# Two-layer recurrent trunk in fp32: half chunks split ahead of the three passages, and a fixed order of the opening

## The chip, the cores and the metric

The kernel runs on one core of one Trainium2 chip. The metric is the device time of one execution in microseconds (us); lower is better. The time before is the median of three runs.

The engines are named as the profile names them: PE (TensorE, matmul) with its weight load PEld, DVE (VectorE), ACT (ScalarE), POOL (GpSimd) and SP (SyncE, which here only issues transfers).

## The reference, cut to what matters

256 tokens of width 2048 pass through two layers. Each layer has a mixer (HGRN2 in the first, gated linear attention in the second) and a squared-ReLU MLP with an inner width of 8192. Each of these four sub-layers is wrapped in the same way: an RMS norm before, an RMS norm with a weight behind, and a residual addition.

```python
def rmsnorm(x, w):
    xf = x.astype(jnp.float32)
    y = xf * lax.rsqrt(jnp.mean(xf * xf, axis=-1, keepdims=True) + NORM_EPS)
    return (y * w.astype(jnp.float32)).astype(x.dtype)

def reference(x, ...):
    ...
    h = x
    for i in range(DEPTH):
        hn = rmsnorm(h, norm_mix_pre[i])
        j = i // N_MIXERS
        if i % N_MIXERS == 0:
            m = hgrn2_mixer(hn, hgrn_w_in[j], lower_bounds[i], hgrn_norm[j], hgrn_w_out[j])
        else:
            m = gla_mixer(hn, gla_w_in[j], gla_w_gk[j], gla_b_gk[j], gla_norm[j], gla_w_out[j])
        h = h + rmsnorm(m, norm_mix_post[i])
        f = sqrelu_mlp(rmsnorm(h, norm_mlp_pre[i]), mlp_w_up[i], mlp_w_down[i])
        h = h + rmsnorm(f, norm_mlp_post[i])
    return h
```

The time goes into the products with the weights, 430 MB of them read once, all in fp32 accuracy.

## The kernel before

**Products.** Activations and weights are split into a high part that the matmul reads exactly (fp32r) and a low remainder. A weight chunk of 1 MB (tile `raw`, three buffers, `load_chunk`, L98) holds two half chunks of 128 x 1024. ACT copies each half into `hi` (L105) and DVE subtracts it from `raw` to give `lo` (L106); the helper is `split`, and the pool `wsp` has five buffers for `hi` and five for `lo`. `mm_half` then does three matmuls of 128x512 for each of the two 128-row slices `k` of a half chunk: high times high (L120), low weight times high activation (L121), high weight times low activation (L122). `gemmT` (L140, L141) does the same with the weights held still, for results that are wanted transposed. The activations of a stage lie in `Xhl` tiles (`xhl`), a high and a low part for each of 16 slices `k` and two token blocks `t` of 128.

**Passages.** `transition` joins the end of one sub-layer to the start of the next; there are three: from the HGRN mixer to its MLP (about 492 us), from the MLP to the attention mixer (about 1212 us), and from that mixer to the last MLP (about 1615 us). A passage has the last of four output quarters (512 columns each) left to multiply. `last(t, j)` is that product for token block `t` and one of the last four half chunks. Then come the post-norm: `first_use` squares the quarter with a running sum (ACT, L278), `rstd` reduces the sums, takes root and reciprocal (DVE L299, ACT L194, DVE L196), `weigh` multiplies a quarter by the norm weight (DVE, L283), and `residual(n, t)` adds the normed quarter `n` to the running tile `h` (DVE, L304). From `h` follow the next activations: `T(t, q)` transposes four 128x128 blocks on PE (L175), ACT writes the high part (L186) and DVE the low part (L188) of four slices `k`. Meanwhile `split_next` splits the first half chunks of the next weights, named N0 to N7 here, and `nxt(t, j)` multiplies them with the new activations. In a passage six of these eight low parts are made on POOL:

```python
        def split_next(eng=G):
```

The second passage has one step more, since the MLP's output is a running sum over groups: `first_use` adds the product to it first (DVE, L343).

**What sets the order.** The code is written for a tile framework whose scheduler orders the instructions of each engine by priority. Inside a `manual_schedule` block the written order holds for the engines named, and only work from outside the block is put between it. Each engine executes its own list strictly in order, and waits there for the tiles it needs. All transfers are issued on SP's queue, in order; an issue waits until the tile's buffer is free. So the transfer for N4 and N5, which takes the raw buffer of the last own half chunk, can be issued once that half is split.

**Opening.** `start` (the first sub-layer) loads the transposed input `xs` and the first weight half chunks in alternation on SP, the very first in two parts of 512 columns, with the input quarters (tile `h`) between the later half chunks; the scheduler orders the computation. `prew` holds the pre-norm weights. `rrow` brings the reciprocal roots of the input's mean squares into a row by two matmuls (tile `psr`); they stand between the second and the third transposed product there.

Of the kernel before, what the change touches and what calls it, by code (L numbers as in the profile page):

```python
# [18 lines left out]
P = 128  # L19
T = 256  # L20
# [10 lines left out]
def trunk(  # L31
# [24 lines left out]
    nc.sync.dma_start(prew, npre)  # L56
# [13 lines left out]
    A.activation(warm, epsb, AF.Sqrt)  # L70
# [30 lines left out]
    def split(raw, eng=None):  # L101

        hi = wsp.tile([P, 1024], F32R, tag="hi", name=nm("hi"))
        lo = wsp.tile([P, 1024], F32R, tag="lo", name=nm("lo"))
        A.activation(hi, raw, AF.Copy)  # L105
        (eng or V).tensor_tensor(lo, raw, hi.bitcast(F32), ALU.subtract)  # L106
        return hi, lo
# [6 lines left out]
    def mm_half(ps, half, hf, xs, t, nk):  # L114

        hi, lo = (w.rearrange("p (k n) -> p k n", k=2) for w in half)
        for kk in range(2):
            k = 2 * hf + kk
            xh, xl = xs(k, t)
            PE.matmul(ps, xh, hi[:, kk, :], start=(k == 0), stop=False)  # L120
            PE.matmul(ps, xh, lo[:, kk, :], start=False, stop=False)  # L121
            PE.matmul(ps, xl, hi[:, kk, :], start=False, stop=(k == nk - 1))  # L122
# [10 lines left out]
    def gemmT(wap, idx, X):  # L133


        ps = psmm.tile([P, 2, T], F32, tag="mm", name=nm("mmT"))
# [62 lines left out]

    def start(which, w, base):  # L200
# [5 lines left out]
        ps = [psmm.tile([P, NB], F32, tag="mm", name=nm("mm")) for _ in range(NT)]  # L206

        def load_h(t, q):
            c = slice(q * NB, (q + 1) * NB)
            nc.sync.dma_start(h[:, t, c], x[t * P:(t + 1) * P, c])  # L210

        def load_half(c, j):
            nc.sync.dma_start(ahead[c][1][:, j, :], w[c].rearrange("p (k n) -> p k n", k=2)[:, j, :])

        with tc.manual_schedule(engines={mybir.EngineType.SP}):
            for hf in range(KT // 2):
# [3 lines left out]
                if hf >= 4:  # L220
                    load_h(0, hf - 4)
                for n in range(2 if hf == 0 else 1):
# [3 lines left out]
                    cs = slice(n * NB, (n + m) * NB)  # L226
                    nc.sync.dma_start(xs[:, ks, :], xT[:, ks, :])
                    nc.sync.dma_start(raw[:, hf % 2, cs], src[:, hf % 2, cs])
# [12 lines left out]
                for t in range(NT):  # L241
                    mm_half(ps[t], half, hf, X, t, KT)
            for q in range(4):
                load_h(1, q)
            nc.sync.dma_start(ident, ident_in)
            for c in range(2):
                ahead[c] = w, wraw.tile([P, 2, 1024], F32, tag="raw", name=nm("raw"))
                for j in range(2):
                    load_half(c, j)
        return X, token_rstd(), ps  # L250

    def token_rstd():
        part = small.tile([P, NT, 4], F32, tag="tp", name=nm("tp"))
        for t in range(NT):
            for q in range(4):
                A.activation(tok(), h[:, t, q * NB:(q + 1) * NB], AF.Square,
                             accum_out=part[:, t, q:q + 1])
# [5 lines left out]
    def rrow(rs):  # L263
        ps = pssc.tile([P, NT, P], F32, tag="sc", name=nm("psr"))
# [6 lines left out]
    class Post:  # L271
# [8 lines left out]
        def weigh(self, ps, n, t):  # L280

            self.mw[n, t] = tok() if ps.space == PSUM else ps
# [6 lines left out]
        def wp(self, n):  # L289
            if ("w", n) not in self.mw:  # L290
                w = tokp.tile([P, NB], F32, tag="wp", bufs=1, name=nm("wp"))
# [10 lines left out]
        def residual(self, n, t):  # L302
            hs = h[:, t, n * NB:(n + 1) * NB]
            V.scalar_tensor_tensor(hs, self.mw[n, t], self.r[t], hs, ALU.mult, ALU.add)  # L304

    ALL = {mybir.EngineType.PE, mybir.EngineType.Activation, mybir.EngineType.DVE,
           mybir.EngineType.Pool}

    def transition(w, base, nk, xs, post, add, which, wn, nbase):
# [15 lines left out]
        raws, N = [], []  # L325
        psn = [psmm.tile([P, NB], F32, tag="mm", name=nm("mm")) for _ in range(NT)]

        def last(t, j):
            mm_half(ps[t], halves[nh - 4 + j], nh - 4 + j, xs, t, nk)

        def split_next(eng=G):
# [3 lines left out]
            N.append(split(raws[-1][:, j % 2, :], eng))  # L335
# [4 lines left out]
        def first_use(t):  # L340
# [5 lines left out]
            return src  # L346

        def T(t, q):
            pt = transpose4(lambda j: h[:, t, q * NB + j * P:q * NB + (j + 1) * P])
            put_split(pt, X, 4 * q, t, lambda j: prew[:, which, 4 * q + j:4 * q + j + 1])  # L350

        post.wp(n)
        with tc.manual_schedule(engines=ALL):
            for j in range(4):
                last(0, j)
            split_next()
            m0 = first_use(0)
            last(1, 0)
            post.rstd(0)
            split_next()  # L360
            post.residual(0, 0)
            post.residual(1, 0)
            last(1, 1)
            split_next()
            post.weigh(m0, n, 0)
            post.residual(2, 0)
            post.residual(3, 0)
            last(1, 2)
            T(0, 0)
            last(1, 3)  # L370
            m1 = first_use(1)
            ss = col()
            V.tensor_reduce(ss, post.part[1], mybir.AxisListType.X, ALU.add)
            T(0, 1)
            post.r[1] = rstd_of(ss, D, 1)
            split_next()
            post.residual(0, 1)
            post.residual(1, 1)
            nxt(0, 0)
            T(0, 2)  # L380
            nxt(0, 1)
            if add is None:
                T(1, 0)
            nxt(0, 2)
            if add is not None:
                T(1, 0)
            T(1, 1)
            nxt(0, 3)
            split_next()
            post.weigh(m1, n, 1)  # L390
# [473 lines left out]
```

## Time and profile before

| quantity | value |
|---|---|
| median of three runs | 2350.85 us (2349.45 to 2351.37) |
| profiled execution, its own time | 2349.59 us |
| its span, first to last instruction | 2347.4 us |
| mean granted clock of PE | 0.996 |
| PE busy | 2320.2 us, 99% of the span |
| PEld, DVE, ACT, POOL busy | 84%, 65%, 51%, 2% |
| read from memory | 429.59 MB, 184 GB/s over the span |
| POOL's half splits | 18, mean 2591 ns |

The profiled execution stands 1.26 us below the median. Its page lists, for each engine, the busy time and its share of the span; groups of instructions give a line of the kernel, the engine, the operation, output and input tiles, the count, and behind the bar the busy time with the mean duration, and the idle time of that engine just before them with what ended it. A timeline row is start and duration in us, the engine, the line, and in brackets the idle time before it and what ended that. The list of waits gives total, number of times and the longest. Window rows give the stretch, its length, and for each engine the busy time with the number of instructions, then PE's granted clock, the busy share of the transfer engines and GB/s.

### The profile page before, as it was taken

To read this page: it belongs to the slowest core of one execution; us is meant where nothing else is said; L and a number is where in the kernel's file an instruction comes from. 1 tells how busy PE (TensorE), PEld (TensorE's weight loads), DVE (VectorE), ACT (ScalarE), POOL (GpSimd) and SP (SyncE) were. 2 spreads that over 40 slices of the span, in tenths; PEclk is the share of its full clock that TensorE was granted. 3 is DMA by queue.
4 is the path that set the end of the run, shared out by engine and by line. 5 is a ranking of instruction groups with operands and counts; after the bars stand their busy time and mean duration, and the time that the engine had idled before them with its cause. 6 is when DMAs were issued, how large, how long until landed. Compare 5 with 4: busy or idle time off the path is not lost.

```text
span 2347.4 us, 29579 instructions
## 1 busy us (share of the span) xinstructions
PE 2320.2 (99%) x11688; PEld 1960.6 (84%) x11688; DVE 1517.2 (65%) x2091; ACT 1197.6 (51%) x1750; POOL 46.7 (2%) x22
## 2 busy tenths in 40 slices
PE   8999999999999999999999999999999999999998
PEld 7888888878888888888878888887888888888887
DVE  6787777566565565565576767656656556556556
ACT  7454554456454454454447456554645445445443
POOL 0000000020000000000010000002000000000000
PEclk9999999999999999999999999999999999999999
DMA  9544545545555555555554544454555555555553
GB/s 320 180 161 163 178 162 178 173 153 203 192 191 186 197 182 195 190 187 194 184 174 156 207 161 163 162 192 167 198 194 183 198 183 194 188 189 189 190 195 139
DMA packets 65867, 433.61 MB, mean 185 GB/s; under 512 B 7968, under 2 KB 8352, under 8 KB 15168
## 3 DMA queue, kind: packets, MB, share of 16 engines
q1 hardware_dynamic: 65728, 431.71, 53.5%
q8 instruction: 92, 1.51, 0.3%
q14 instruction: 47, 0.39, 0.0%
HBM read 429.59 MB, written 2.10 MB: 184 GB/s over the span
## 4 chain that ended last, share of the span: by engine, by line
PE 96%; DVE 3%; ACT 0%; DMA 0%; SPq 0%; issue 0%; DVEq 0%; ACTq 0%
PE mmT L140 27%; PE mm L121 17%; PE mm L122 17%; PE mm L120 17%; PE mmT L141 14%; PE sc L506 2%; DVE h L304 2%; PE tr L175 1%; DVE xhl L188 1%; PE sd L541 0%; PE po L590 0%; PE po L593 0%; PE po L592 0%; DVE tok L283 0%; DMA raw<-w_hin 0%; ACT xhl L186 0%
## 5 line engine op out<-in xcount | busy, mean ns | idle before, releaser
L106 DVE TENSOR_TENSOR lo<-raw,hi 128x1024 fp32r<-128x1024 f32 x776 | 948.7, 1225 | 711.7 <-ACT hi L105 710.4
L105 ACT ACTIVATE hi<-raw 128x1024 fp32r<-128x1024 f32 x794 | 839.5, 1060 | 986.2 <-PE mm L122 577.5
L140 PE MATMUL mmT<-xhl,hi 128*128 128x512 f32 x2704 | 952.8, 397 | 0.1
L141 PE MATMUL mmT<-xhl,lo 128*128 128x256 f32 x2704 | 761.5, 282 | 0.8 <-DVE lo L106 0.8
L122 PE MATMUL mm<-hi,xhl 128*128 128x512 f32 x1856 | 726.3, 392 | 7.4 <-DVE xhl L188 7.4
L120 PE MATMUL mm<-hi,xhl 128*128 128x512 f32 x1856 | 727.7, 394 | 5.6 <-ACT hi L238 5.6
L121 PE MATMUL mm<-lo,xhl 128*128 128x512 f32 x1856 | 726.8, 392 | 0.4 <-DVE lo L239 0.4
L140 PEld LDWEIGHTS mmT<-xhl,hi 128*128 128x128 f32 x2704 | 507.3, 188 | 121.7 <-issue 1.3
L141 PEld LDWEIGHTS mmT<-xhl,lo 128*128 128x128 f32 x2704 | 510.8, 189 | 3.1 <-DVE lo L106 1.1
L122 PEld LDWEIGHTS mm<-hi,xhl 128*128 128x128 f32 x1856 | 350.0, 189 | 81.8 <-DVE xhl L188 8.7
L120 PEld LDWEIGHTS mm<-hi,xhl 128*128 128x128 f32 x1856 | 350.1, 189 | 77.8 <-ACT hi L238 6.3
L121 PEld LDWEIGHTS mm<-lo,xhl 128*128 128x128 f32 x1856 | 350.3, 189 | 73.0 <-issue 1.0
L106 POOL TENSOR_TENSOR lo<-raw,hi 128x1024 fp32r<-128x1024 f32 x18 | 46.5, 2591 | 1592.3 <-ACT hi L105 1581.5
L149 DVE TENSOR_TENSOR half<-mmT,half 128x256 f32<-128x256 f32 x169 | 70.6, 418 | 0.0
L447 DVE TENSOR_TENSOR tok<-tok,mm 128x512 f32<-128x512 f32 x108 | 69.0, 680 | 0.0
L148 ACT COPY half<-mmT 128x256 f32<-128x256 f32 x169 | 59.7, 354 | 0.0
L433 DVE SCALAR_TENSOR_TENSOR half<-half,rr 128x256 f32<-128x256 f32 x120 | 51.0, 425 | 4.2
L436 ACT ACTIVATE half<-half 128x256 f32<-128x256 f32 x120 | 50.3, 419 | 3.7
L437 DVE TENSOR_TENSOR xhl<-half,xhl 128x256 fp32r<-128x256 f32 x120 | 50.2, 419 | 0.0
L435 ACT ACTIVATE xhl<-half 128x256 fp32r<-128x256 f32 x120 | 48.0, 400 | 0.0
L304 DVE SCALAR_TENSOR_TENSOR h<-tok,col,h 128x512 f32<-128x512 f32 x32 | 47.8, 1531 | 0.3
L570 DVE TENSOR_TENSOR qk<-qk,tt 128x256 f32<-128x256 f32 (+1 forms) x96 | 46.6, 517 | 1.7 <-ACT kc L524 1.7
(132 smaller groups left out, 777.6 us busy)
## 6 DMA issues: line engine op xcount, KB each, us to landing
raw<-w_up SPq DMA_DIRECT2D x128, 1024.0 KB, 4.8
raw<-w_dn SPq DMA_DIRECT2D x128, 1024.0 KB, 4.8
raw<-w_hin SPq DMA_DIRECT2D x58, 1024.0 KB, 4.8
raw<-w_gin SPq DMA_DIRECT2D x48, 1024.0 KB, 4.8
raw<-w_hout SPq DMA_DIRECT2D x16, 1024.0 KB, 4.8
raw<-w_gout SPq DMA_DIRECT2D x16, 1024.0 KB, 5.0
raw<-w_hin SPq DMA_DIRECT2D x11, 512.0 KB, 7.1
wp<-npost SPq DMA_DIRECT2D x16, 256.0 KB, 3.4
```

Of the source, the lines that this page charges most:

```text
L105: A.activation(hi, raw, AF.Copy)
L106: (eng or V).tensor_tensor(lo, raw, hi.bitcast(F32), ALU.subtract)
L120: PE.matmul(ps, xh, hi[:, kk, :], start=(k == 0), stop=False)
L121: PE.matmul(ps, xh, lo[:, kk, :], start=False, stop=False)
L122: PE.matmul(ps, xl, hi[:, kk, :], start=False, stop=(k == nk - 1))
L140: PE.matmul(ps, hi[:, kk * P:(kk + 1) * P], X.both(k), start=(k == 0), stop=False)
L141: PE.matmul(ps[:, 0, :], lo[:, kk * P:(kk + 1) * P], X.both(k)[:, 0, :], start=False, stop=(k == KT - 1))
L148: A.copy(u, ps[:, 1, :])
L149: V.tensor_tensor(u, ps[:, 0, :], u, ALU.add)
L304: V.scalar_tensor_tensor(hs, self.mw[n, t], self.r[t], hs, ALU.mult, ALU.add)
L433: V.scalar_tensor_tensor(u, u, 0.0, rr[0], ALU.max, ALU.mult)
L447: V.tensor_tensor(m[n, t], m[n, t], ps[t], ALU.add)
```

## The change

**Passages.** POOL is no longer used. `split` is cut into `split_hi` (ACT) and `split_lo` (DVE), and six of the next stage's half chunks (N0 to N5) are split ahead of the passage's block. Their parts lie in spare tiles, which the generator `spares` hands out: the feature tiles `qk`, `f` and `tt` (N0, N1), the accumulators (N2), the ordinary pool (N3) and one buffer of `big` (N4, N5). `first_use` now also weighs the quarter. The transposes (`T_in`) and their copies (`T_out`) are separate steps, and PE's order is written anew: all of `nxt(0, j)` stands inside the block, and `nxt(1, j)` follows it.

**Opening.** The order in `start` is written out for all engines. The first `xs` goes first on SP, the first weight part goes on ACT's queue, `prew` comes second; four matmuls on a constant run first on PE; the first half chunk is multiplied slice by slice; the first four transposed products are issued there (`next_chunk`), and the input quarters are loaded among their chunks. `rrow` comes behind the four.

**Weight quarter.** The last quarter of the post-norm weight (`wp(3)`) has a tile of its own and is loaded before the passage.

```diff
-    def split(raw, eng=None):
...
+    def split_hi(raw, into=None):
+        hi, lo = into or (wsp.tile([P, 1024], F32R, tag="hi", name=nm("hi")),
+                          wsp.tile([P, 1024], F32R, tag="lo", name=nm("lo")))
         A.activation(hi, raw, AF.Copy)
-        (eng or V).tensor_tensor(lo, raw, hi.bitcast(F32), ALU.subtract)
         return hi, lo
+
+    def split_lo(raw, half):
+        V.tensor_tensor(half[1], raw, half[0].bitcast(F32), ALU.subtract)
...
+    def spares():
+        def take(pool, tag, shape):
+            return pool.tile(shape, F32R, tag=tag, name=nm(f"s{tag}"))
+
+        qk = take(featp, "qk", [P, 2, 1024])
+        yield qk[:, 0, :], qk[:, 1, :]
+        yield take(featp, "f", [P, 1024]), take(featp, "tt", [P, 1024])
+        yield take(accp, "accA", [P, 1024]), take(accp, "accB", [P, 1024])
+        yield None
+        b = take(big, "big", [P, 4, 1024])
+        for j in range(2):
+            yield b[:, 2 * j, :], b[:, 2 * j + 1, :]
+        while True:
+            yield None
...
+        def input_quarters(t, qs):
+            for q in qs:
+                c = slice(q * NB, (q + 1) * NB)
+                nc.sync.dma_start(h[:, t, c], x[t * P:(t + 1) * P, c])
+            for q in qs:
+                square(part, t, q)
+
+        def next_chunk(c):
+            raw = wraw.tile([P, 2, 1024], F32, tag="raw", name=nm("raw"))
+            for j in range(2):
+                nc.sync.dma_start(raw[:, j, :], w[c].rearrange("p (k n) -> p k n", k=2)[:, j, :])
+            ahead[c] = w, raw
+            early.append(gemmT(w, c, X, *((psmm, "mm") if c < 2 else (pssc, "sc"))))
+
+        with tc.manual_schedule(engines=ALL | {mybir.EngineType.SP}):
...
                     nc.sync.dma_start(xs[:, ks, :], xT[:, ks, :])
-                    nc.sync.dma_start(raw[:, hf % 2, cs], src[:, hf % 2, cs])
+                    (nc.scalar if first else nc.sync).dma_start(raw[:, hf % 2, cs], src[:, hf % 2, cs])
+                    if first:
+                        nc.sync.dma_start(prew, npre)
+                        A.activation(warm, epsb, AF.Sqrt)
+                        for _ in range(4):
+                            idle = pstr.tile([P, T], F32, tag="tr", name=nm("idle"))
+                            PE.matmul(idle, bc(epsb, [P, P]), bc(epsb, [P, T]), start=True, stop=True)
...
+            next_chunk(0)
+            next_chunk(1)
+            input_quarters(0, (0, 1))
+            next_chunk(2)
+            input_quarters(0, (2, 3))
             nc.sync.dma_start(ident, ident_in)
...
+            next_chunk(3)
+            input_quarters(1, range(4))
+            rs = rstd_sum(part)
...
+                w = (tok() if n == 3 else
+                     tokp.tile([P, NB], F32, tag="wp", bufs=1, name=nm("wp")))
...
             post.square(src, n, t)
-            return src
+            post.weigh(src, n, t, tok())
...
         post.wp(n)
+        for _ in range(6):
+            split_next()
         with tc.manual_schedule(engines=ALL):
             for j in range(4):
                 last(0, j)
+            first_use(0)
+            last(1, 0)
+            last(1, 1)
+            post.rstd(0)
+            split_next_hi()
+            post.residual(0, 0)
+            last(1, 2, (0,))
+            T_in(0, 0)
+            post.residual(1, 0)
+            post.residual(2, 0)
+            T_out(0, 0)
+            last(1, 2, (1,))
+            last(1, 3)
...
+            nxt(0, 3)
+            split_next_lo()
...
+            T_out(1, 0)
             split_next()
...
-        for t in range(NT):
-            for j in range(4, 8):
-                nxt(t, j)
+        for j in range(KT // 2):
+            nxt(1, j)
```

DVE's order at the first passage, before. `lo` rows are splits of the passage's own last half chunks, the row with `col` and `pp` is the reduction of the squares, `mm` is the last quarter's product, `wp` the norm weight.

```order
L106 TENSOR_TENSOR lo_4225<-raw_4222,hi_4224 128x1024
L106 TENSOR_TENSOR lo_4229<-raw_4222,hi_4228 128x1024
L299 TENSOR_REDUCE col_4278<-pp_3696 128x1
L196 RECIPROCAL col_4282<-col_4280 128x1
L304 SCALAR_TENSOR_TENSOR h<-tok_3838,col_4282,h 128x512
L304 SCALAR_TENSOR_TENSOR h<-tok_3986,col_4282,h 128x512
L283 TENSOR_TENSOR tok_4302<-mm_4142,wp_4236 128x512
L304 SCALAR_TENSOR_TENSOR h<-tok_4134,col_4282,h 128x512
```

And now; `sqk`, `stt`, `saccB` and `sbig` are the low parts of N0, N1, N2 and of N4 and N5 in their spare tiles, `lo_4256` is N3's.

```order
L106 TENSOR_TENSOR sqk_4242<-raw_4240,sqk_4242 128x1024
L106 TENSOR_TENSOR stt_4246<-raw_4240,sf_4245 128x1024
L106 TENSOR_TENSOR lo_4229<-raw_4226,hi_4228 128x1024
L106 TENSOR_TENSOR lo_4233<-raw_4226,hi_4232 128x1024
L106 TENSOR_TENSOR saccB_4252<-raw_4249,saccA_4251 128x1024
L106 TENSOR_TENSOR lo_4256<-raw_4249,hi_4255 128x1024
L106 TENSOR_TENSOR sbig_4261<-raw_4259,sbig_4261 128x1024 x2
L333 TENSOR_TENSOR tok_4294<-mm_4146,tok_3996 128x512
L350 TENSOR_REDUCE col_4308<-pp_3698 128x1
L218 RECIPROCAL col_4312<-col_4310 128x1
L355 SCALAR_TENSOR_TENSOR h<-tok_3840,col_4312,h 128x512
```

The six splits, which were on POOL or behind, now stand ahead of the weighing, the reduction and the first residual step in DVE's queue.

On ACT the same place reads now as follows; `tok,pp<-mm` is the squaring of the last quarter, `hi_4316` is N6's, the `xhl` rows are the copies of the transposes.

```order
L102 ACTIVATE saccA_4251<-raw_4249 128x1024
L102 ACTIVATE hi_4255<-raw_4249 128x1024
L102 ACTIVATE sbig_4261<-raw_4259 128x1024 x2
L328 ACTIVATE tok_4292,pp_3698<-mm_4146 128x512
L216 ACTIVATE col_4310<-col_4308,epsb 128x1
L102 ACTIVATE hi_4316<-raw_4314 128x1024
L208 ACTIVATE xhl_4236<-tr_4323,prew 128x128 x4
```

The squaring of the last quarter comes behind the high parts of N4 and N5.

SP's queue at the opening, before (`xs` transposed input, `raw` weights, `h` input quarters):

```order
L56 DMA prew<-npre 128x64
L227 DMA xs<-xT 128x256
L228 DMA raw_115<-w_hin 128x512
L227 DMA xs<-xT 128x256
L228 DMA raw_115<-w_hin 128x512
L227 DMA xs<-xT 128x512
L228 DMA raw_115<-w_hin 128x1024
```

And now:

```order
L260 DMA xs<-xT 128x256
L263 DMA prew<-npre 128x64
L260 DMA xs<-xT 128x256
L261 DMA raw_114<-w_hin 128x512
L260 DMA xs<-xT 128x512
L261 DMA raw_114<-w_hin 128x1024
```

The first `raw` has left SP's queue for ACT's, and `prew` stands behind the first `xs`. The input quarters, which followed from the fourth half chunk on, now stand among the chunks of the transposed products.

More of the change, by code (lines that the diff above doesn't have):

```diff
@@ L112, in split_chunk, with mm_half @@
         return [split(raw[:, hf, :]) for hf in range(2)]
-    def mm_half(ps, half, hf, xs, t, nk):
+    def mm_half(ps, half, hf, xs, t, nk, kks=(0, 1)):
         hi, lo = (w.rearrange("p (k n) -> p k n", k=2) for w in half)
-        for kk in range(2):
+        for kk in kks:
             k = 2 * hf + kk
@@ L206, in start @@
         ps = [psmm.tile([P, NB], F32, tag="mm", name=nm("mm")) for _ in range(NT)]
[L208 to L215, printed above, removed]
+        early = []
+        part = small.tile([P, NT, 4], F32, tag="tp", name=nm("tp"))
+        def input_quarters(t, qs):
[11 more added lines that the diff above has]
+        with tc.manual_schedule(engines=ALL | {mybir.EngineType.SP}):
             for hf in range(KT // 2):
@@ L240, in start, with square @@
                                     half[0][:, cs].bitcast(F32), ALU.subtract)
-                for t in range(NT):
-                    mm_half(ps[t], half, hf, X, t, KT)
-            for q in range(4):
-                load_h(1, q)
-            nc.sync.dma_start(ident, ident_in)
[L246 to L250, printed above, removed]
+                    if hf == 0:
+                        for t in range(NT):
+                            mm_half(ps[t], half, hf, X, t, KT, (n,))
+                if hf:
+                    for t in range(NT):
+                        mm_half(ps[t], half, hf, X, t, KT)
+            next_chunk(0)
[3 more added lines that the diff above has]
+            input_quarters(0, (2, 3))
+            nc.sync.dma_start(ident, ident_in)
+            next_chunk(3)
+            input_quarters(1, range(4))
+            rs = rstd_sum(part)
+        return X, rs, ps, early
+    def square(part, t, q):
+        A.activation(tok(), h[:, t, q * NB:(q + 1) * NB], AF.Square, accum_out=part[:, t, q:q + 1])
     def token_rstd():
@@ L496, in scores @@
         kt = 4 // nh
-        cmb = accp.tile([P, nh, P], F32, tag="cmb", name=nm("cmb"))
-        acc = [accp.tile([P, nh, P], F32, tag=f"acc{t}", name=nm("acc")) for t in range(NT)]
-        accX = accp.tile([P, nh, P], F32, tag="accX", name=nm("accX"))
+        accs = accp.tile([P, NT, nh, P], F32, tag="accA", name=nm("acc"))
+        acc = [accs[:, t] for t in range(NT)]
+        rest = accp.tile([P, 2, nh, P], F32, tag="accB", name=nm("rest"))
+        accX, cmb = rest[:, 0], rest[:, 1]
         tt = featp.tile([P, 1024], F32, tag="tt", name=nm("tt"))
@@ L613, in hgrn @@
     def hgrn(then):
-        X, rs, ps0 = start(0, w_hin, 32)
+        X, rs, ps0, first = start(0, w_hin, 32)
         v = {}
@@ L655, in hgrn @@
             qk, f = qkf()
-            early = []
             if g == 0:
-                early = [gemmT(w_hin, j, X) for j in range(2)]
                 rr = rrow(rs)
             for j in range(4):
-                ps = early[j] if j < len(early) else gemmT(w_hin, 4 * g + j, X)
+                ps = gemmT(w_hin, 4 * g + j, X) if g else first[j]
                 u = fold(ps, rr)
```

128 lines of the change are left out of this document (59 added, 69 removed).

## The prediction

> **What bounds the kernel now.** I read the page's busy line first, then a table of windows for the stages, the list of PE's waits, and the timeline at the places that these two name.
>
> ```profile
> PE 2320.2 (99%) x11688; PEld 1960.6 (84%) x11688; DVE 1517.2 (65%) x2091; ACT 1197.6 (51%) x1750; POOL 46.7 (2%) x22
> ```
> ```profile
> 26.00:484.00 458.00, 456.02 (x2423) 391.61 (x2422) 344.98 (x550) 244.40 (x350) 0.00 (x0) 1.00 0.53 182
> 500.00:516.00 16.00, 14.20 (x63) 11.19 (x64) 15.07 (x32) 8.89 (x25) 7.71 (x4) 0.89 0.35 129
> ...
> 1220.00:1230.00 10.00, 7.74 (x25) 5.83 (x26) 8.15 (x18) 5.02 (x16) 2.39 (x1) 0.68 0.22 69
> ```
> ```profile
> PE mm L122 <- DVE xhl L188: 7.4, 3, 3.4
> PE mm L120 <- ACT hi L238: 5.6, 1, 5.6
> PE tr L175 <- DVE h L304: 2.2, 4, 1.0
> ...
> PE tr L175 <- DVE xhl L188: 1.0, 1, 1.0
> ```
>
> PE (matmul) is busy for 2320.2 of 2347.4 us, so all that a reordering can win is some 27 us of idle, and what the lowered clock costs beside it. The window rows give length, busy time of PE, PEld, DVE, ACT, POOL, then PE's granted clock. A steady stage (26 to 484 us) is full. The passages are not: from 500 to 516 us PE is busy 14.2 of 16 at a clock of 0.89, and DVE 15.07; in the second passage 7.74 of 10 at 0.68. The waits (total, times, longest) say the same: besides the first load (5.6), nearly all waiting is on DVE's `h` and `xhl`: three long waits of 7.4 together, 2.2 and 1.0, all in passages. A quarter of a per cent of the time is 5.9 us; 0.2% (4.7 us) is about what a measurement of this kernel can tell from no change.
>
> **What the first passage loses.** PE's matmuls there, and the DVE row ahead of the wait:
>
> ```profile
> 498.89 0.40 PE L121 MATMUL mm<-lo,xhl 128*128 128x512 f32 x1
> 501.28 0.50 PE L122 MATMUL mm<-hi,xhl 128*128 128x512 f32 x1 [2.00 <-DVE xhl L188]
> 502.67 0.67 PE L120 MATMUL mm<-hi,xhl 128*128 128x512 f32 x1
> 503.14 0.63 PE L121 MATMUL mm<-lo,xhl 128*128 128x512 f32 x1
> ...
> 505.98 0.58 PE L120 MATMUL mm<-hi,xhl 128*128 128x512 f32 x1
> 506.39 0.39 PE L121 MATMUL mm<-lo,xhl 128*128 128x512 f32 x1
> ...
> 513.69 0.66 PE L175 MATMUL tr<-ident,h 128*128 128x128 f32 x4 [0.41 <-DVE h L304]
> ```
> ```profile
> 495.89 5.07 DVE L304 SCALAR_TENSOR_TENSOR h<-tok,col,h 128x512 f32<-128x512 f32 x2
> ```
>
> ```profile
> 492.09 0.39 PE L122 MATMUL mm<-hi,xhl 128*128 128x512 f32 x1
> ...
> 492.32 0.39 PE L120 MATMUL mm<-hi,xhl 128*128 128x512 f32 x1
> ```
>
> Starts of 128x512 matmuls stand 0.23 us apart when PE runs freely (the last two rows). In the first rows 2.39 lie between 498.89 and 501.28, a loss of 2.16. From 502.67 to 505.98 the starts are 0.43 apart (cold): six steps lose 1.2 and the transposes between them 0.36. The waits ahead of the transposes at 507.82 and 513.69 lose 0.3 and 0.6, odds and ends 0.1. Sum 4.75 us. The two `h` steps ahead of the wait took 5.07, since GpSimd splits at the same time (below). The third passage has the same rows 1123 us later: also 4.75.
>
> The second passage:
>
> ```profile
> 1214.51 0.60 PE L175 MATMUL tr<-ident,h 128*128 128x128 f32 x4
> ...
> 1217.00 0.40 PE L121 MATMUL mm<-lo,xhl 128*128 128x512 f32 x1
> 1220.85 0.80 PE L122 MATMUL mm<-hi,xhl 128*128 128x512 f32 x1 [3.45 <-DVE xhl L188]
> ...
> 1226.13 0.53 PE L120 MATMUL mm<-hi,xhl 128*128 128x512 f32 x1
> 1226.50 0.39 PE L121 MATMUL mm<-lo,xhl 128*128 128x512 f32 x1
> ...
> 1228.20 0.66 PE L175 MATMUL tr<-ident,h 128*128 128x128 f32 x4 [0.38 <-DVE h L304]
> 1229.90 0.66 PE L175 MATMUL tr<-ident,h 128*128 128x128 f32 x4 [1.04 <-DVE xhl L188]
> ```
>
> The wait costs 3.6 (3.85 less 0.23), the cold stretch to 1226.50 another 2.7, the two short waits 0.55 and 1.35, and a last wait on `h` of 1.0 (the longest of the third list row) 1.2 with its restart: 9.5 us with 0.1 of small losses. All three passages lose 19.0.
>
> **The change part by part.** GpSimd's 18 half splits go away. What they do to DVE, and the durations for the new order:
>
> ```profile
> L304 DVE SCALAR_TENSOR_TENSOR h<-tok,col,h x32: 739/754/2933, 494.0 to 2343.5; 128x512 f32<-128x512 f32 x32
> ```
> ```profile
> L106 DVE TENSOR_TENSOR lo<-raw,hi 128x1024 fp32r<-128x1024 f32 x776 | 948.7, 1225 | 711.7 <-ACT hi L105 710.4
> L105 ACT ACTIVATE hi<-raw 128x1024 fp32r<-128x1024 f32 x794 | 839.5, 1060 | 986.2 <-PE mm L122 577.5
> ```
> ```profile
> 481.26 5.77 SPq L98 DMA_DIRECT2D raw<-w_up  x2
> ```
> ```profile
> 1199.43 5.77 SPq L98 DMA_DIRECT2D raw<-w_gin  x2
> ```
> ```profile
> raw<-w_up SPq DMA_DIRECT2D x1, 1024.0 KB, 4.9
> ```
> ```profile
> 492.52 0.60 ACT L278 ACTIVATE tok<-mm 128x512 f32<-128x512 f32 x1 [4.38 <-PE mm L122]
> 493.24 0.16 DVE L299 TENSOR_REDUCE col<-pp 128x1 f32<-128x4 f32 x1 [6.56 <-ACT tok L278]
> 493.96 1.42 DVE L304 SCALAR_TENSOR_TENSOR h<-tok,col,h 128x512 f32<-128x512 f32 x2
> 495.29 0.69 DVE L283 TENSOR_TENSOR tok<-mm,wp 128x512 f32<-128x512 f32 x1
> ```
>
> An `h` step takes 0.71 alone (1.42 for two) and up to 2.93 beside a GpSimd split. SBUF — State Buffer in the Trainium skill ("SBUF: two separate sides") says that GpSimd and a DVE operation with two SBUF inputs take one shared port pair as an exclusive lock, the loser waiting for the whole instruction; the row of 739/754/2933 fits it, and by it all eight `h` of a passage come down to 0.7.
>
> *The six splits ahead.* They stand on ACT and DVE in front of the statistics, the eight `h` and the transposes' copies. N0 to N3 come early. N4 and N5 do not: their chunk is the second of the two loads of the row 481.26 (5.77 long, an issue being 0.33, so it issues at 486.70, when the raw buffer of the last own half is free). The landing row gives 4.9; the N6 chunk is issued right behind it, so I take 5.0: 491.7. Then ACT splits two halves (1.03 each) to 493.8, DVE, one behind, to 495.15 (1.17 each, back to back); the weighing is done at 495.85 (0.69), the reduction, root and reciprocal, 0.72 from 493.24 to 493.96, at 496.55, and the first `h` at 497.25. PE's first transpose, after 15 matmuls behind 492.32 instead of 18, is ready at 495.7. Stall about 1.6 us where before there was none at this place. From there on I followed the order row by row: the eight `h` at 0.7, each group of four lower-half copies at 1.1, four DVE splits, and PE's own 0.23 per matmul. No later PE instruction waits, the nearest by 0.4 us. So 4.75 becomes 1.6, if the clock stays: it dropped after 2.00 of idle, and not after 0.38 and 1.04 within 2.3 us (1.42 together). 1.6 is nearer the latter, so no drop; with it, 1.6 more. Bounds of the stall: 0 (landing 1.6 sooner) and 4.4 (landing 2.8 later, last row below). Gain 3.15, and 3.15 again in the third passage.
>
> TensorE: Matmul & The Clock Gate in the Trainium skill ("Part 1: The HAM clock gate") lowers the clock after an idle window of about 3.4 us and asks for no gap over about 3 us. Here 2.00 us was enough, so the row decides; by the rule the sum would be the same for 1.6 and would not fear a stall of 2.5.
>
> *The second passage.* The same chunk issues at 1204.87 (row 1199.43, the second of two) and lands at 1209.9. Behind it DVE has more: two splits to 1213.3, the weighing of the third quarter to 1214.0, the addition to the running sum (0.7) 1214.7, the last weighing 1215.4, statistics, and `h` at 1217.0. PE's first transpose, at 1214.51 before, is ready 3 matmuls sooner, 1213.8. Stall 3.2; next to the 3.45 that was followed by a cold stretch of 2.7, so I add 2.4. Loss 5.6 for 9.5: gain 3.9, bounds 9.5 (no stall) and 1.0 (stall 2.8 longer).
>
> *The opening.* Ahead of the point from which PE runs without a wait stand:
>
> ```profile
> 1.18 0.42 SPq L227 DMA_DIRECT2D xs<-xT  x1
> 1.65 0.42 SPq L228 DMA_DIRECT2D raw<-w_hin  x1
> ...
> 9.78 1.06 ACT L238 ACTIVATE hi<-raw 128x1024 fp32r<-128x1024 f32 x1 [0.36 <-DMA raw<-w_hin]
> ...
> 12.15 0.50 PE L121 MATMUL mm<-lo,xhl 128*128 128x512 f32 x1 [0.36 <-DVE lo L239]
> ```
>
> ACT waits for the second half chunk. The loads ahead of it are issued 0.47 us apart on SP (1.18, 1.65); one of them now goes through ACT's queue and `prew` comes second, so everything lands one slot, 0.47, sooner. PE has one matmul more left at 12.15 than in the old order (0.23 less to win). The issue on ACT's queue (0.42 on SP) pushes ACT's start-up, table load and one root, back by as much, which ends before the first data. Net gain 0.3; bounds 1.2 (two slots and the interleaved matmuls count) and -0.5 (ACT's queue starts late). The four idle matmuls run before the first data; their end can cost only if it comes after 6.5, from where 12 cold matmuls (0.43 each) still end before 11.7. The input's loads move behind the first chunks; the statistics they feed are due on PE some 50 us in, after four transposed products (16 steps of 0.34 each, 5.4 a product), and by their landing order are ready near 44.
>
> *The rest.* The weight quarter in its own tile is loaded earlier; no row of PE's waits names it, so nothing. The 18 low halves that move from GpSimd to DVE (1.2 each, 22 us in all) are covered, since DVE is free 35% and the six ahead run while PE still works on its own last halves. Renamed accumulators: nothing.
>
> Sum 0.3 + 3.15 + 3.9 + 3.15 = 10.5 us. The profiled execution took 2349.59, 1.26 under the median of 2350.85: 2339.1 on its scale, 2340.3 on the median's.
>
> **Rivals.** *(a) No stall at the first transposes.* The loads come sooner than the issue rows say, or DVE's queue is not held: all 19.0 and the opening, 2331.5. Against it: the raw buffer is freed by the same split as before.
>
> *(b) The stalls go cold everywhere*, with landings of 5.4 to 6: passages lose 3.6, 7.3 and 3.6, gain 4.8 with the opening: 2346. For it: 2.00 us sufficed.
>
> *(c) Slower: the chunk ahead lands late.* The N6 chunk and the next one now follow within 3 us. In the opening a chunk behind another landed after:
>
> ```profile
> raw<-w_hin SPq DMA_DIRECT2D x1, 1024.0 KB, 7.7
> ```
>
> With 7.7 for N4's chunk the stalls are 4.4, 6.0 and 4.4, each followed by a cold stretch of 2.7: 7.1 + 8.7 + 7.1 against 19.0, less 0.3: 3.6 us slower, 2354.5. It decides from a landing of about 6.6 us on, where gain and loss cancel. Against it: the chunk is first in the queue, the follower second, and the 7.7 was a follower's.
>
> *(d) Only the opening works* and the passages merely exchange their waits one for one: 2350.5.
>
> **How the numbers follow.** Forecast 0.55 (its own range 2336 to 2344, which holds a drop of the clock in one or both of the short stalls), (a) 0.14, (b) 0.17, (c) 0.07, (d) 0.07. Faster by over 0.2% (under 2346.1): the forecast, (a) and over half of (b), 0.79. Slower by over 0.2% is only the far part of (c): 0.05. Same: 0.16. The range 2331 to 2348 leaves out (c), (d) and the edge of (a).
>
> **What would show it.** Right: `h` at 0.7 us each in the passages; PE waits named `tr` on `h` of about 1.6, 3.2 and 1.6 us near 497, 1216 and 1619, no wait of `mm` on the lower-half copies, a clock near 1 in the first and third passage; the first long run of matmuls from 11.7. Wrong: a wait on the lower-half copies in the middle of a passage (DVE's queue is then too long), N4's split starting long before or after 491.7, or a low clock behind the short stalls.

## The result, and the profile after

The changed kernel takes 2335.41 us (median of four runs, 2334.62 to 2336.27) against 2351.11 of the kernel before on the same chip: ratio 0.9935, 95% interval 0.9918 to 0.9952. It is faster by 15.7 us; forecast were 10.5, from 2350.85 to 2340.3. The profiled execution is the slowest of the four, 2336.27, with a span of 2334.4; beside the profiled one of before (2349.59, near the fastest of its kernel) the span is 13.0 shorter and the execution's own time 13.3.

PE's waits after the change (total, times, longest):

```profile
PE tr L197 <- DVE h L355: 2.5, 2, 1.5
PE mm L142 <- ACT hi L277: 1.9, 2, 1.4
PE mm L143 <- DVE lo L278: 1.2, 3, 0.8
PE tr L197 <- DVE tok L759: 1.1, 1, 1.1
PE idle L267 <- DVE one L65: 0.9, 1, 0.9
```

The three waits of 7.4 us on the lower-half copies (`xhl`) are gone; what is left in the passages are two waits on `h`, 2.5 together. Two windows of the passages, as before, and the residual steps:

```profile
500.00:516.00 16.00, 16.00 (x83) 13.20 (x82) 13.86 (x33) 9.76 (x29) 0.00 (x0) 1.00 0.26 78
...
1220.00:1230.00 10.00, 8.46 (x42) 6.76 (x41) 8.59 (x20) 6.33 (x16) 0.00 (x0) 1.00 0.05 9
```
```profile
L355 DVE SCALAR_TENSOR_TENSOR h<-tok,col,h x32: 736/744/752, 495.1 to 2330.4; 128x512 f32<-128x512 f32 x32
```

From 500 to 516 us PE is busy all the time at the full clock (14.2 and 0.89 before), and no residual step takes more than 0.752 us (2.933 before).

How much each stage gave is read from the issue of one and the same weight chunk ahead of each passage, first before, then after:

```profile
475.82 0.33 SPq L98 DMA_DIRECT2D raw<-w_up  x1
...
1193.99 0.33 SPq L98 DMA_DIRECT2D raw<-w_gin  x1
...
1598.82 0.33 SPq L98 DMA_DIRECT2D raw<-w_up  x1
```
```profile
476.36 0.33 SPq L96 DMA_DIRECT2D raw<-w_up  x1
...
1190.87 0.33 SPq L96 DMA_DIRECT2D raw<-w_gin  x1
...
1589.38 0.33 SPq L96 DMA_DIRECT2D raw<-w_up  x1
```

The changed kernel is 0.54 behind ahead of the first passage, 3.12 ahead in front of the second, 9.44 in front of the third, and 13.0 at the end. So the stretches with the passages gave 3.7, 6.3 and 3.6 us, and the opening with the first mixer lost 0.5 in this execution.

### The profile page after: what moved, and what is told of

It reads as the page before. It is cut to its first block, busy times and chain, and to the rows that moved or that the text cites. A ratio compares the mean times of both kernels' runs of the same rounds, so it can differ in the third digit from the quotient of the medians.

```text
span 2334.4 us, 29573 instructions
## 1 busy us (share of the span) xinstructions
PE 2318.3 (99%) x11696; PEld 1958.8 (84%) x11696; DVE 1507.2 (65%) x2109; ACT 1198.5 (51%) x1751; POOL 0.2 (0%) x4
## 4 chain that ended last, share of the span: by engine, by line
PE 98%; DVE 1%; DMA 0%; ACT 0%; issue 0%; SPq 0%; DVEq 0%; ACTq 0%
PE mmT L162 27%; PE mm L143 18%; PE mm L142 18%; PE mm L144 18%; PE mmT L163 14%; PE sc L568 2%; PE tr L197 1%; PE sd L603 0%; PE po L652 0%; PE po L655 0%; PE po L654 0%; DMA raw<-w_hin 0%; DMA raw<-w_gin 0%; PE pg L785 0%; DVE h L355 0%; DVE xhl L210 0%
## 5 line engine op out<-in xcount | busy, mean ns | idle before, releaser
L102 ACT ACTIVATE hi<-raw 128x1024 fp32r<-128x1024 f32 x779 | 824.3, 1061 | 975.9 <-PE mm L144 577.4
L142 PE MATMUL mm<-hi,xhl 128*128 128x512 f32 x1796 | 702.4, 392 | 1.9 <-ACT hi L277 1.9
L143 PE MATMUL mm<-lo,xhl 128*128 128x512 f32 x1796 | 701.8, 391 | 1.2 <-DVE lo L278 1.2
L144 PE MATMUL mm<-hi,xhl 128*128 128x512 f32 x1796 | 699.9, 390 | 0.0
L142 PEld LDWEIGHTS mm<-hi,xhl 128*128 128x128 f32 x1796 | 337.5, 188 | 72.8 <-ACT hi L277 3.3
L143 PEld LDWEIGHTS mm<-lo,xhl 128*128 128x128 f32 x1796 | 337.7, 188 | 71.7 <-DVE lo L278 2.2
L144 PEld LDWEIGHTS mm<-hi,xhl 128*128 128x128 f32 x1796 | 337.5, 188 | 70.6 <-issue 0.5
L568 PEld LDWEIGHTS sc<-qk,kc 128*128 128x128 f32 x288 | 37.9, 191 | 2.3
L568 PE MATMUL sc<-qk,kc 128*128 128x128 f32 x288 | 38.3, 276 | 0.0
```

The costliest lines, as they stand in the source:

```text
L568: PE.matmul(ps[:, hd, :], l(hd * kt + k), r(hd * kt + k), start=(k == 0), stop=(k == kt - 1))
```

## The experiments

**Halves of the change.** First the new passages (with the weight quarter's tile) on the old opening: `start`, its loads and the first products are those of before.

> The changed kernel with the old opening: new passages and the weight quarter's own tile, but start, its load order and the first transposed products as before. In the changed kernel's trace PE stands 1.4 us later at the end of the first product than before (matmuls cold from 12.0 to 15.4 us, granted clock 0.90), gets 0.9 back where the old opening waited at 32 us, and is 0.4 behind at 94 us. Theory 'the opening costs': without it the time is 0.4 to 0.6 us under the changed kernel, 2334.9, with all of the gain kept. Rival, the forecast's term: the opening gains 0.3, so 2335.7. Both expect no PE wait in the first and third passage and two in the second (1.0 and 1.5 us).

Measured: 2334.55 us, ratio to before 0.9933 (0.9920 to 0.9947). PE's waits in the passages are two on `h`, as in the changed kernel:

```profile
PE tr L199 <- DVE h L332: 2.7, 2, 1.5
```

In the time, the passages alone give the whole gain, and the opening adds nothing that can be told from zero. The parts do not simply add up, though. The same chunks are issued here at

```profile
476.62 0.33 SPq L98 DMA_DIRECT2D raw<-w_up  x1
...
1190.17 0.33 SPq L98 DMA_DIRECT2D raw<-w_gin  x1
...
1588.80 0.33 SPq L98 DMA_DIRECT2D raw<-w_up  x1
```

which is 0.8 behind the kernel before, then 3.8 and 10.0 ahead; at the end (span 2332.6) it is 14.7. The stretches with the passages gave 4.6, 6.2 and 4.7 us, in the first and third about one more than in the changed kernel, with the same instructions there. And the opening is 0.8 late although it is that of before. Both come from the step of the transposed products, taken up below.

The other half: the new opening alone, with the old passages and GpSimd.

> The kernel before with the new opening alone; passages with GpSimd as before. Theory 'the opening costs': 2351.1 plus 0.4 to 0.6, 2351.6, with cold matmuls from 12 to 15.4 us in the trace. Rival (forecast): 2350.8, PE running without a wait from 11.7. The three long passage waits (2.0, 3.45, 2.0 us) stay by both.

Measured: 2349.06 us (eleven runs, 2348.16 to 2352.73), ratio 0.9998 (0.9989 to 1.0007). The long waits of the passages stayed, as both said. The cold stretch of the first theory did not come, and PE's last wait of the opening ended at 11.2. Windows from 12 to 26 us, first of the changed kernel's first trace, then of this kernel, then of the changed kernel run once more (below):

```profile
12.00:26.00 14.00, 13.99 (x56) 11.46 (x57) 11.26 (x22) 13.00 (x20) 0.00 (x0) 0.90 1.03 361
```
```profile
12.00:26.00 14.00, 14.00 (x63) 11.58 (x62) 10.74 (x21) 12.87 (x21) 0.00 (x0) 1.00 0.99 372
```
```profile
12.00:26.00 14.00, 14.00 (x63) 11.43 (x62) 10.76 (x21) 13.25 (x21) 0.00 (x0) 1.00 0.98 374
```

The clock was 0.90 in the first and 1.00 in the other two, with the same order of instructions: 56 matmuls against 63 in the 14 us. In the first trace the clock was up early and PE then starved:

```profile
10.75 0.51 PE L142 MATMUL mm<-hi,xhl 128*128 128x512 f32 x1 [1.38 <-ACT hi L277]
12.01 0.79 PE L143 MATMUL mm<-lo,xhl 128*128 128x512 f32 x1 [0.75 <-DVE lo L278]
12.60 0.63 PE L144 MATMUL mm<-hi,xhl 128*128 128x512 f32 x1
```

So the cold stretch (0.63 a matmul, to 14.7) is one execution's course and not the order's fixed price; my theory for both runs falls. The first chunk of the MLP is issued at 474.19 here, 1.6 us sooner than before, and the trace stays ahead by about as much to its end; the times of the eleven runs do not tell that from zero.

The first passage of this kernel shows something more:

```profile
499.64 0.50 PE L144 MATMUL mm<-hi,xhl 128*128 128x512 f32 x1 [1.99 <-DVE xhl L210]
```
```profile
500.00:516.00 16.00, 13.85 (x72) 10.93 (x71) 15.08 (x33) 8.74 (x25) 7.58 (x3) 1.00 0.31 91
```

It is the wait of 2.00 of the kernel before, but no low clock follows (1.00 for 0.89). PE then waits 1.73 at the transposes of 506.21 instead, and the stretch with the passage is as long as before to 0.1 us. By this trace DVE's chain sets the length of the old passage, and the cold matmuls only fill time in which PE would have waited.

The changed kernel again, unaltered:

> The changed kernel itself, unaltered, beside the two others on one chip: 2335.4 within 1 us by every theory; whether its opening shows the cold stretch from 12 to 15.4 us again (it did in the first trace, not in the opening alone) tells whether that is the order's doing or the execution's.

Measured: 2334.41 us, ratio 0.9932 (0.9920 to 0.9945), and the full clock from 12 us on. Here the matmuls stand 0.43 apart until 9.67, so the low clock came earlier, at a place where PE waits in the other traces, and PE's last wait there ends at 11.2. Its first chunk of the MLP is issued at 474.24, 2.1 us sooner than in the first trace and 1.6 sooner than before, and its span is 2332.3, 2.1 less than the first profiled one.

**The idle matmuls.**

```diff
-                        for _ in range(4):
-                            idle = pstr.tile([P, T], F32, tag="tr", name=nm("idle"))
-                            PE.matmul(idle, bc(epsb, [P, P]), bc(epsb, [P, T]), start=True, stop=True)
```

> The changed kernel without the four idle matmuls on a constant at the start of PE; nothing of the computation is left out. Theory 'too early': they bring the clock up near 5.2 us, so that PE starves (1.4 and 0.75 us of idle at 9 to 12 us) and the clock falls for 12.0 to 15.4, just when the loads have caught up; without them the first matmuls run cold, fill that starved time, and PE is at full clock from about 12, as in the kernel before: 1.5 us faster, 2333.9. Rival 'starvation decides': the same loads leave the same idle time, the clock is low at 12 anyhow: no change, 2335.4, or up to 1 us slower.

Measured: 2334.79 us, ratio 0.9933 (0.9921 to 0.9946). Between the changed kernel's 2335.41 and 2334.41, so the four matmuls have no effect that these times can tell. Without them PE's matmuls are cold until about 9.4 and its last wait there ends at 11.7; with them that wait ended at 12.0 in the first trace and at 11.2 in the second, where the clock was low until 9.7 in spite of them.

**GpSimd alone.** The kernel before, its six low parts on DVE, in the old place:

```diff
-        def split_next(eng=G):
+        def split_next(eng=V):
```

> The kernel before with one word changed: the six low parts of a passage are made on DVE, in the old place, instead of GpSimd. Theory 'contention': the residual steps slowed by GpSimd (up to 2.9 us each against 0.74) made the waits, so most of the passages' 16 us goes: about 2340. Rival 'place': the low parts (1.2 us each) now stand between the residual steps in DVE's own queue; in the first passage three of them and the four residual steps end near 501 us, as late as the 500.9 of before, so the waits stay: about 2351, within 2 us.

Measured: 2345.94 us, ratio 0.9979 (0.9970 to 0.9988): 4.6 us faster, between the two theories.

```profile
L304 DVE SCALAR_TENSOR_TENSOR h<-tok,col,h x32: 742/746/752, 496.4 to 2340.3; 128x512 f32<-128x512 f32 x32
```
```profile
PE tr L175 <- DVE h L304: 5.2, 6, 1.5
PE mm L122 <- DVE xhl L188: 3.1, 3, 1.1
```

The residual steps are fast (0.746), so the slowness beside GpSimd was GpSimd's doing. But PE still waits for DVE: 3.1 on the copies where it had been 7.4, and 5.2 on `h` where it had been 2.2, and DVE now makes the low parts between. Taking GpSimd out of the old order is thus worth about 5 of the 16 us, net of the time that its splits cost in DVE's queue; the two were not measured apart.

**The six splits ahead.** The changed kernel, with N0 to N5 split inside the block, between the residual steps, in the same spare tiles (high parts on ACT, low parts on DVE):

```diff
-        for _ in range(6):
-            split_next()
...
             post.rstd(0)
-            split_next_hi()
+            split_next()
...
             post.residual(1, 0)
+            split_next()
             post.residual(2, 0)
...
```

> The changed kernel, but N0 to N5 are split inside the passage's block, one at a time between the residual steps and the copies, still on DVE and in the same spare tiles; PE's order is unchanged. Theory 'ahead': the six splits (1.2 us each on DVE) are worth their place; inside the block they push the residual steps and copies back, N4's low part comes near 509 in the first passage where PE wants it near 506.7, so 3 to 5 us of waits return per passage: 2343 to 2350. Rival 'PE's order': with all of nxt(0, j) inside the block PE has enough to do, and GpSimd gone is the rest: at most 2338.

Measured: 2354.18 us, ratio 1.0018 (1.0009 to 1.0027): 19 us slower than the changed kernel and slower than before.

```profile
PE mm L142 <- ACT sbig L102: 6.1, 3, 2.0
PE tr L197 <- DVE h L355: 4.3, 3, 1.6
PE mm L143 <- DVE sbig L106: 2.5, 3, 0.8
```

PE waits in each passage for N4's parts (`sbig`, 2.0 and 0.8 us) and for `h`, a little worse than I had put it, with cold matmuls behind. The longest of these waits, 6.1 in all, is for ACT's high parts, which stand behind the copies of T(0,3) here, so the run prices this placement on both engines and not DVE's load alone. With the splits in these places the new order of PE is worth less than the old one, so it does not bring the gain by itself; other places inside the block were not tried.

**The weight quarter's tile.** The changed kernel with the last quarter back in the shared tile:

```diff
-                w = (tok() if n == 3 else
-                     tokp.tile([P, NB], F32, tag="wp", bufs=1, name=nm("wp")))
+                w = tokp.tile([P, NB], F32, tag="wp", bufs=1, name=nm("wp"))
...
-        post.wp(3)
         down(NG - 1)
...
-            if n == 2:
-                post.wp(3)
```

> The changed kernel with the last post-norm weight quarter back in the shared single tile, loaded where it was. Theory 'shared tile now matters': in the second passage the third quarter is weighed at 1208.2 to 1208.9, so the load of the last quarter (3.4 to 4.8 us) ends at 1212.3 to 1213.7, where the changed kernel weighs at 1209.5: a wait 3 to 4 us longer there, with or without a cold stretch of 2 to 3: 2338 to 2342. Rival, the forecast's 'no wait names it, so nothing': 2335.4.

Measured: 2341.58 us, ratio 0.9962 (0.9946 to 0.9977): 6 to 7 us slower than the changed kernel, all in the stretch with the second passage, which here takes 0.9 more than before instead of 6.3 less.

```profile
1212.19 0.69 DVE L333 TENSOR_TENSOR tok<-tok,wp 128x512 f32<-128x512 f32 x1 [4.37 <-DMA wp<-npost]
```
```profile
PE tr L197 <- DVE h L354: 6.7, 2, 5.1
```

DVE sits idle 4.37 us for the load that could only be issued once the third quarter was weighed, and PE then 5.1 for `h` (1.0 in the changed kernel); a cold stretch adds the rest (clock 0.79 from 1214 to 1222). The theory that the tile matters in the new order holds.

**What was left in the second passage.** The changed kernel with two residual steps moved up:

```diff
             T_in(0, 3)
+            post.residual(0, 1)
             T_out(0, 3)
             nxt(0, 2)
-            post.residual(0, 1)
             nxt(0, 3)
-            split_next_lo()
             post.residual(1, 1)
+            split_next_lo()
```

> The changed kernel with two residual steps moved up in the passages: h(0,1) ahead of the copies of T(0,3), h(1,1) ahead of N6's low part. Theory 'order on DVE': the second of the two waits left in the second passage (1.5 us at 1224.3, on h(0,1), which stands behind 1.1 us of copies that PE needs only later) goes: 1.5 us faster, 2333.9. Rival 'DVE is the bound there': the wait moves to the next transposes and nothing is won, 2335.4.

Measured: 2333.04 us, ratio 0.9927 (0.9914 to 0.9939), 1.4 to 2.4 under the changed kernel.

```profile
PE tr L197 <- DVE h L355: 1.1, 1, 1.1
```

One of the two waits on `h` is gone and none has come in its place. The intervals of the two ratios overlap, so it is this row, not the time, that shows it; by the chunk rows the stretch with the second passage gave 7.9 us for the changed kernel's 6.3, and the other two gave what they gave there.

**The transposed products.** The stretch of the first passage lost 4.8 us of waits and cold steps but gave only 3.7. The rest is further on, where PE never waits. A transposed product has 16 pairs of matmuls (512 and 256 columns) and one weight chunk, so chunks are issued one product apart; before, then after:

```profile
556.86 0.33 SPq L98 DMA_DIRECT2D raw<-w_up  x1
...
562.40 0.33 SPq L98 DMA_DIRECT2D raw<-w_up  x1
```
```profile
558.60 0.33 SPq L96 DMA_DIRECT2D raw<-w_up  x1
...
564.26 0.33 SPq L96 DMA_DIRECT2D raw<-w_up  x1
```

5.54 us a product before, 5.66 after, through the first eleven or so products of the MLP: 1.2 us, and again behind the third passage. Per pair that is about 347 and 353 ns. The same two steps occur in both kernels elsewhere. The kernel with the new passages alone is the check; there two neighbouring chunks are issued at

```profile
553.06 0.33 SPq L98 DMA_DIRECT2D raw<-w_up  x1
...
558.61 0.33 SPq L98 DMA_DIRECT2D raw<-w_up  x1
```

5.55 apart, the faster step, and its first and third stretch gave 4.6 and 4.7, nearly all of the loss of 4.75 that the prediction had counted. In its opening the eight transposed products from 33 to 78 us take the slower step, 354 ns for 347 before, which is the 0.8 us that it is late. So neither the order of the passages nor that of the opening sets the step by itself; the kernels may also differ in where their tiles lie, and no run tests that. The first try to force the faster one swaps the start of each product:

```diff
-                PE.matmul(ps, hi[...], X.both(k), ...)
-                PE.matmul(ps[:, 0, :], lo[...], ...)
+                if c == 0 and kk < 2:
+                    high(kk)
+                    if kk:
+                        low(0)
+                        low(1)
+                else:
+                    high(kk)
+                    low(kk)
```

> The changed kernel with the first four matmuls of each transposed product in the order high, high, low, low instead of high, low, high, low; same work. In the traces a pair (512 and 256 columns) steps at 347 ns in some stretches and at 353 in others, each stretch keeping its step until other matmuls come between; before, the first two groups of both MLPs ran at 347 behind a place where two 512-column matmuls followed each other, and at 353 in the changed kernel, which took 1.1 us of the gain at each. Theory 'phase': the swap sets the faster step everywhere, 2200 pairs by 6 ns, 13 us: 2322. Rival 'position': the step hangs on something else (buffers, banks), and the swap costs what the two short matmuls in a row take, 0 to 0.06 us each in 168 products: 2335 to 2345.

Measured: 2333.62 us, ratio 0.9929 (0.9916 to 0.9943).

```profile
651.97 0.62 PE L162 MATMUL mmT<-xhl,hi 128*128 128x512 f32 x2
652.43 0.40 PE L166 MATMUL mmT<-xhl,lo 128*128 128x256 f32 x2
652.67 0.40 PE L162 MATMUL mmT<-xhl,hi 128*128 128x512 f32 x1
...
653.73 0.40 PE L162 MATMUL mmT<-xhl,hi 128*128 128x512 f32 x1
```

The step did not hold: behind the swap (from 652.67) three pairs take 1.06 us, 353 ns each. The two swapped pairs took 0.70 us instead of 0.71; 168 times that hundredth is under 2 us, and the time lies 0.8 to 1.8 under the changed kernel's two medians, which does not tell it from zero. The theory of a phase that a kick sets falls; whether the order within the pairs matters was the next question. Then all eight of the high part ahead of all eight of the low part:

```diff
             for kk in range(8):
                 k = 8 * c + kk
                 PE.matmul(ps, hi[:, kk * P:(kk + 1) * P], X.both(k), start=(k == 0), stop=False)
+            for kk in range(8):
+                k = 8 * c + kk
                 PE.matmul(ps[:, 0, :], lo[:, kk * P:(kk + 1) * P], X.both(k)[:, 0, :],
```

> The changed kernel with each transposed product's matmuls grouped within a half chunk: the eight of the high weight part (512 columns), then the eight of the low part (256 columns); same matmuls, another order. With the swapped start, high-high-low-low stepped 236, 226, 114 and 119 ns, 695 for two pairs where the alternating order takes 707, and matmuls of 512 columns in a row step at 227 elsewhere. Theory 'alternation costs': in a group of eight the steps come to 227 and 113, 340 a pair for 347 to 353, 2704 pairs by 8 to 13 ns: 20 to 33 us faster, 2303 to 2315. Rival 'weight loads': short matmuls in a row cannot hide the 188 ns weight load in front of each, eight in a row step near 190: 60 to 75 ns more per pair, 2500 or more. Against it: 128-column matmuls step at 112 with a load each.

Measured: 2323.80 us, ratio 0.9887 (0.9872 to 0.9902), 10.6 under the changed kernel run beside it (2334.41). The direction is the first theory's, the size half of its lower end.

```profile
651.03 1.12 PE L165 MATMUL mmT<-xhl,lo 128*128 128x256 f32 x8
651.99 2.00 PE L162 MATMUL mmT<-xhl,hi 128*128 128x512 f32 x8
653.83 0.40 PE L165 MATMUL mmT<-xhl,lo 128*128 128x256 f32 x2
```

The starts of the groups give the steps: eight short matmuls 0.96 (120 ns each, not 113), eight long ones 1.84 (230, not 227): 350 a pair, 3 to 4 ns under the 353 of most of the 2704 pairs, some 8 us. One us more is the wait on `tok` (1.1 in the list above, in the first mixer), which does not occur in this kernel; what is left of the 10.6 was not traced. The short matmuls step at 120 ns with a weight load of 188 each, so they do hide these loads and the rival falls.

With the two residual steps and without the idle matmuls:

> The changed kernel with the grouped transposed products, the two residual steps moved up, and without the four idle matmuls. Theory: the gains add, 2.4 us (residual steps) and 0.6 (idle matmuls, as in their own runs) under the grouped one. Rival: the grouped products want their low parts later and the waits of the second passage move, so that it is equal to the grouped one within 1 us.

Measured: 2321.98 us, ratio 0.9879 (0.9866 to 0.9893), 1.8 under the grouped one, where the theory had 3.0 and the rival at most 1. And in twos:

> The combined kernel (residual steps moved up, no idle matmuls) with the transposed products in twos, two of the high part and then two of the low part, instead of eights. In the eights the short matmuls step at 114 once and then 119 to 120, the long ones at 227 to 236: 349 a pair. In twos the swapped start showed 236, 226, 114, 119: 695 for two pairs, 347.5. Theory 'short runs are cheap': 1.5 ns by 2704 pairs, 4 us faster than the combined kernel's 2322.0: 2318. Rival: kept up over a whole product the step settles near 352 as in the alternating order: 2330.

Measured: 2321.72 us, ratio 0.9881 (0.9864 to 0.9897): equal to the eights; the step is about the same there.

```profile
650.03 0.62 PE L162 MATMUL mmT<-xhl,hi 128*128 128x512 f32 x2
...
652.81 0.40 PE L162 MATMUL mmT<-xhl,hi 128*128 128x512 f32 x1
```

Eight pairs, from the first row to the last, take 2.78 us, 348 ns each, 2 ns less than in eights, but the wait on `tok` is back; neither theory's number came. The best two of these kernels are 28 us under the kernel before, and 12 under the changed one.

## Why the prediction was right, and where it was off

*Right in kind.* The gain comes from the passages, PE's waits on the lower-half copies go, the residual steps fall to 0.74, and no wait takes their place in the middle of the first and third passage. The median lies in the stated range, half a microsecond under the forecast's own narrower one, towards rival (a). The single terms were further off than the total.

*First and third passage: the step on N4's chunk failed.* The prediction let it issue at 486.70, "when the raw buffer of the last own half is free". It issued 2 us sooner:

```profile
483.44 1.22 DVE L106 TENSOR_TENSOR stt<-raw,sf 128x1024 fp32r<-128x1024 f32 x1
```
```profile
484.69 0.33 SPq L96 DMA_DIRECT2D raw<-w_up  x1
```
```profile
489.65 2.01 ACT L102 ACTIVATE sbig<-raw 128x1024 fp32r<-128x1024 f32 x2 [0.98 <-DMA raw<-w_up]
```

N1's low part ends at 484.66, and its chunk's buffer is the one that N4's takes: splitting N0 and N1 early frees a buffer earlier too, which the old rows could not show and I had not followed. That this transfer takes the buffer of the last own half chunk is so only in the order of before. The list of SP's waits names N1's low part in all three passages:

```profile
SPq L96 <- DVE stt L106: 7.8, 3, 2.8
```

The landing of 4.9 was right (ACT starts on the chunk at 489.65). N4 and N5 are then split by 493.1, before the last product's squaring is done, and the first transpose at 496.26 waits for nothing. The stall of 1.6 was 0, the loss of 4.75 went whole: for these two passages that is rival (a), and the argument against it, that the same split frees the buffer, is what was wrong. Of these 4.75 only 3.7 and 3.6 reached the time, since the transposed products behind these two passages fell into the slower step, a term that the sum did not have; in the kernel with the passages alone, where they kept the faster one, 4.6 and 4.7 did. That 3.7 and 3.6 stand so near the forecast's 3.15 is luck: the stall that did not come and the slower step that did nearly cancel.

*Second passage: the stall was over-sized.* Forecast 3.2 with a cold stretch, 5.6 in all. Measured:

```profile
1211.83 0.66 PE L197 MATMUL tr<-ident,h 128*128 128x128 f32 x4 [0.96 <-DVE h L355]
...
1224.30 0.65 PE L197 MATMUL tr<-ident,h 128*128 128x128 f32 x4 [1.54 <-DVE h L355]
```

The chunk came earlier here too, so the first wait is 0.96. The second, of 1.54, was not forecast: `h` of the second block stood behind the copies of T(0,3) on DVE, as the run with the two steps moved up shows. Neither was followed by a low clock. Gain 6.3 for 3.9.

*Opening: not to be told from zero in the times,* for a forecast of 0.3. PE ran without a wait from 12.0, not 11.7, in the first trace, which had the cold stretch and lost 0.5 up to the first passage. In the two traces of this order without that stretch PE ran from 11.2 and the first passage came 1.6 sooner than before, more than the forecast's bound of 1.2. The earlier start is 0.9 of it (12.15 before). A wait that the sum did not have is another 0.8, in the list of PE's waits before, at 32.9 us; it is gone:

```profile
PE mmT L141 <- DVE lo L106: 0.8, 1, 0.8
```

The slower step of the products there takes 0.8 back; the rest was not taken apart.

*The weight quarter: "nothing" was wrong.* That no row of the old waits named it was true and did not matter: the new order weighs the last quarter ahead of the first `h`, and there the tile is worth 6 to 7 us.

*GpSimd's 18 splits were covered on DVE,* as forecast, where they stand ahead of the passage. In the two orders that had them between the residual steps they were not: in the old one PE still waited 5.2 and 3.1 us for DVE, though the kernel was faster than before, and in the new one, with the high parts moved too, it was slower. Rivals (b), (c) and (d) did not happen.

## What to carry to other kernels

A step that is moved ahead also frees its buffer ahead: follow the buffer to the next transfer before putting a landing time into a chain. When an order is rewritten, ask of each small load in it what now stands directly behind it; the old list of waits cannot say. And a fully busy engine can still lose time per instruction: compare the step of the same work in different stretches.

## What the runs showed of the hardware

- Alternating matmuls of 512 and 256 columns step at 347 or at 353 ns a pair, and stay in one or the other for whole stretches; what sets it was not found. Twos and eights of each kind step at 348 to 350 in the MLPs, and the eights made the changed kernel 10.6 us faster than the alternating order, in which most stretches stood at 353.
- The clock fell after 1.38 and 0.75 us of idle within 3 us, and in the kernel before after 2.00; it did not after 1.54 or 0.96 alone, nor after 1.99 in the kernel with the opening alone (1.00 from 500 to 516 us, against 0.89 before). So a wait of 2 us can lower it and need not. TensorE: Matmul & The Clock Gate in the Trainium skill ("Part 1: The HAM clock gate") speaks of an idle window of about 3.4 us; these runs show that less than that can suffice.
- A residual step on DVE with both inputs in SBUF takes 0.74 us with GpSimd quiet, never more than 0.753 in any of these runs, and up to 2.93 beside its splits.
